# A hybrid trunk layer: the row tiles of the last two attention heads and of the output projection, taken from the last to the first

## The chip, the cores and the metric

One NeuronCore of a Trainium2 chip runs the whole kernel; nothing is shared with other cores. The metric is the device time of one execution in microseconds (us). Of the kernel before there are three timed runs with a median of 576.46 us (576.36 to 576.82), and one profiled execution.

TensorE (PE) multiplies, VectorE (DVE), ScalarE (ACT) and GpSimd (POOL) do the element-wise work, and SyncE (SP) issues the transfers. Each engine works through its own list of instructions in the order in which they were written down, and waits where a result of another engine is not there yet.

## What is computed

One layer over 1024 positions of width 1024, batch 1, everything in 32-bit floats:

```
h    = rms_norm(x) * gain * (1 + scale(c)) + shift(c)
proj = h @ w_in                       # 1024 x 3328: state-space, 4 diff heads, sliding-window heads, gates
y    = concat( s5(u)             * silu(z_ssm),      # 256 columns
               diff_attention(q, k, v) * silu(z_diff),   # 4 heads x 128 columns
               sliding_window(q, k, v) * silu(z_swa) )   # 256 columns
out  = rms_norm(x + gate(c) * (y @ w_out))
```

A differential head takes two softmaxes over the same causal rows and subtracts them:

```
p = softmax(q1 k1' / 8 + bias) - lam * softmax(q2 k2' / 8 + bias)    # causal: query t sees keys 0..t
o = rms_norm(p @ v) * gain
```

Query tile i (128 positions) sees i + 1 key tiles, so tile 7 has eight times the keys of tile 0. Each tile of each head is independent of the others; a tile of `out` needs that tile of y from all heads.

## The kernel before

The program text is Python that writes the five instruction lists once, in an order that a small planner sets. A `Model` keeps an estimated clock for each engine and each tile. Every stage that belongs to attention, state space or epilogue is a generator; it yields what it waits for, and a `Mixer` resumes one when the model says that its inputs are there. TensorE's long matrix products (`proj`, the output projection) call `mix.tick()` between groups of three matmuls, and in these places the generators put their instructions. So the order on every engine depends on the model's clocks, and moving one stage moves many instructions. All instructions go through one helper, so the profile gives line 109 for all of them; the tiles' names tell them apart.

Products are exact to nearly 32 bits: an operand is split into a high and a low part (`woh` and `wol` of the output weights, `yh` and `yl` of y), and three matmuls go to each product.

The projections run in a fixed order, ending with z2, q3, k3, z3 (gate of head 2, queries and keys of head 3, gate of head 3). After a head's keys, `diff(h, i, ...)` is put in the mixer for its eight query tiles ("rows" below, i + 1 key tiles each); at most three rows of a head are under way. A row's steps and names:

- `pS`: scores on TensorE, in one or two pieces of up to 512 keys for each of the two softmaxes, four matmuls for a piece of both
- `sp`: DVE adds the bias and takes the row maximum in one pass per piece, ACT takes the exponential, DVE combines the two softmaxes
- `pdT`, `dT`: i + 1 transposes on TensorE, copied out by ACT (first four) and DVE (the rest)
- `pdO`: the product with v; `do`, `oo`: copy and square on ACT, then three small instructions on POOL (`dmx`), then DVE scales `do`
- `pdy`: transpose on TensorE, after which DVE multiplies the gate into `z`, which now holds this row of y

During z3, `on_k(k)` splits the output weights one 128-row tile after the other, in the order `KO`: ACT makes `woh`, and POOL (four tiles, in pieces of 256 columns) or DVE makes `wol`. The first two y tiles are loaded there too (`load_y`, six 128 x 128 pieces and the residual x) and split (`split_y`): six eighths come from memory, the last two eighths directly from the gates `z` of heads 2 and 3, once `DF[h]["done"]` counts enough rows.

The output projection runs in eight row tiles of two halves of 512 columns (the last tile in 512, 256, 256); up to three halves are open at once, and the loop takes one whose next eighth is ready. Where none is, it opens another or steps the mixer. A half takes 24 matmuls (`po`), eight times `woh*yh`, `wol*yh`, `woh*yl`. `epilogue` adds gate and residual on DVE (`res`), takes the norm and stores the tile.

What sets the order around the change is this loop with the mixer, the row counter `st["run"]` of each head and `done`, which the projection waits on.

Of the kernel before, what the change touches and what calls it, by code (L numbers as in the profile page):

```python
# [16 lines left out]
D = 1024  # L17
NT = 8
# [211 lines left out]
def body(ctx, tc, x, c, norm_gain, ada_w, ada_b, w_in, w_out, lam_re, lam_im, log_step,  # L230
# [45 lines left out]
    def when(cond):  # L276
        return lambda: 0.0 if cond() else 1e9
# [150 lines left out]
    PW = {}  # L428
# [890 lines left out]

    DF = {h: {"run": 0, "done": 0} for h in range(4)}  # L1320

    def diff(h, i, q, k, store, width):
        st = DF[h]
        yield (when(lambda: st["run"] == i and i - st["done"] < width and f"vn{h}" in VN and h in PW.get("bd", ())),
               k[0], k[1], k[2], k[3], q[1], VN.get(f"vn{h}", k[3]), bank("ps"))
        vn = VN[f"vn{h}"]
        bias = PW["bd"][h]
        if i == 6 and h < 3:
            PW["bd"][h + 1] = page(f"bd{h + 1}")
            g_scale(PW["bd"][h + 1], bias, 0.5)  # L1330
        ncol = (i + 1) * 128
        qs = slice(i * 128, (i + 1) * 128)
        if i < 4:
            t = page("sp", (128, 2, 512))
            sp = [t[:, m] for m in range(2)]
        else:
            sp = [page(f"sp{m}") for m in range(2)]
        mx = sml.tile([128, 8], F32, name="dmx", bufs=8)
        nch = (ncol + 511) // 512
        w = (i + 1 + nch - 1) // nch * 128  # L1340
        for a in range(nch):
            for m in range(2):
                if a or m:
                    yield (bank("ps"),)
                c0, c1 = a * w, min(ncol, (a + 1) * w)
                p = pst("ps", "pS")
                scores(p[:, :c1 - c0], q, k, m, qs, slice(c0, c1))
                o = 896 - 128 * i
                V.tensor_tensor_reduce(sp[m][:, c0:c1], p[:, :c1 - c0], bias[:, o + c0:o + c1], 0.125,
                                       -1e38 if a == 0 else mx[:, m:m + 1], OP.add, OP.max, mx[:, m:m + 1])  # L1350
                rel(p)
        st["run"] += 1
        V.tensor_scalar(mx[:, 2:4], mx[:, 0:2], -1.0, None, op0=OP.mult)
        yield (mx,)
        for m in range(2):
            A.activation(sp[m][:, :ncol], sp[m][:, :ncol], AF.Exp, bias=mx[:, 2 + m:3 + m],
                         accum_out=mx[:, 4 + m:5 + m])
        yield (sp[1], mx)
        V.reciprocal(mx[:, 6:8], mx[:, 4:6])
        V.scalar_tensor_tensor(mx[:, 0:1], mx[:, 7:8], mx[:, 4:5], nl, op0=OP.mult, op1=OP.mult)  # L1360
        V.scalar_tensor_tensor(sp[0][:, :ncol], sp[1][:, :ncol], mx[:, 0:1], sp[0][:, :ncol],
                               op0=OP.mult, op1=OP.add)
        pT = page("dT_", (128, 8, 128))
        for b0 in range(0, i + 1, 4):
            nb = min(4, i + 1 - b0)
            yield (sp[0], bank("pt"))
            p = pst("pt", "pdT", (128, 4, 128))
            for a in range(nb):
                PE.transpose(p[:, a], sp[0][:, (b0 + a) * 128:(b0 + a + 1) * 128], ident)
            if b0 == 0:  # L1370
                A.activation(pT[:, b0:b0 + nb], p[:, :nb], AF.Copy)
            else:
                V.tensor_copy(pT[:, b0:b0 + nb], p[:, :nb])
            rel(p)
        yield (pT, bank("po"))
        p = pst("po", "pdO", (128, 128))
        for a in range(i + 1):
            PE.matmul(p, lhsT=pT[:, a], rhs=vn[:, a], start=(a == 0), stop=(a == i))
        yield (p,)
        o = sml.tile([128, 128], F32, name="do", bufs=5)  # L1380
        oo = sml.tile([128, 128], F32, name="oo", bufs=2)
        A.activation(o, p, AF.Copy)
        rel(p)
        A.activation(oo, o, AF.Square, scale=mx[:, 6:7], accum_out=mx[:, 1:2])
        rsqrt(mx[:, 2:3], mx[:, 1:2], 128)
        G.tensor_tensor(mx[:, 3:4], mx[:, 2:3], mx[:, 6:7], OP.mult)
        yield (mx, "V")
        V.tensor_scalar(o, o, mx[:, 3:4], None, op0=OP.mult)
        yield (when(lambda: "z" in st),)
        z = st["z"]  # L1390
        yield (o, bank("pt"), z)
        p = pst("pt", "pdy", (128, 128))
        PE.transpose(p, o, ident)
        yield (p,)
        V.scalar_tensor_tensor(z[:, qs], p, subh, z[:, qs], op0=OP.mult, op1=OP.mult)
        rel(p)
        st["done"] += 1
        if store and st["done"] == NT:
            SP.dma_start(ycat[2 + h], z)
# [67 lines left out]
    def load_y(i):  # L1467
        t = page("yt", (128, 6, 128))
        for j, k in enumerate(KO[:6]):
            SP.dma_start(t[:, j], ycat[k][:, i * 128:(i + 1) * 128])  # L1470
        YT[i] = t
        XR[i] = page("xr")
        SP.dma_start(XR[i], dap(x, i * 128 * D, [[D, 128], [1, D]]))

    def split_y(i):

        yield (YT[i], when(lambda: i < 2 or DONE["po"] >= i - 1)) + (("A", "V") if i else ())
        t = YT.pop(i)
        hi = page("yh", (128, 8, 128), F32R)
        lo = page("yl", (128, 8, 128), F32R)  # L1480
        A.activation(hi[:, 0:6], t, AF.Copy)
        V.tensor_sub(lo[:, 0:6], t, hi[:, 0:6].bitcast(F32))
        SPL[i] = [hi, lo, [mdl.w[lo.tensor.name]] * 6]
        for j in range(2):
            yield (when(lambda: 2 + j in YD and DF[2 + j]["done"] > i),)
            yield (YD[2 + j],)
            y = YD[2 + j][:, i * 128:(i + 1) * 128]
            A.activation(hi[:, 6 + j], y, AF.Copy)
            V.tensor_sub(lo[:, 6 + j], y, hi[:, 6 + j].bitcast(F32))
            SPL[i][2].append(mdl.w[lo.tensor.name])  # L1490
# [57 lines left out]
    def epilogue(i, pp):  # L1548

        r = page("res")  # L1550
        ss2 = sml.tile([128, 4], F32, name="fs")
        jk = page("jk2")
        for n in range(2):
            cs_ = slice(n * 512, (n + 1) * 512)
            yield (when(lambda: len(pp) > n and DONE["n"] >= 2 * i + n + 1),)
            yield (pp[n], XR[i])
            tts(r[:, cs_], pp[n], gate["g"][:, cs_], OP.mult)
            DONE["h"] += 1
            tts(r[:, cs_], r[:, cs_], XR[i][:, cs_], OP.add)
            yield (r, "A")  # L1560
            A.activation(jk[:, cs_], r[:, cs_], AF.Square, accum_out=ss2[:, n:n + 1])
        yield (ss2,)
        tts(ss2[:, 2:3], ss2[:, 0:1], ss2[:, 1:2], OP.add, G)
        G.tensor_scalar(ss2[:, 2:3], ss2[:, 2:3], D * EPS, None, op0=OP.add)
        tts(ss2[:, 3:4], ss2[:, 2:3], mhalf, OP.pow, G)
        for n in range(2):
            yield (ss2, "V")
            cs_ = slice(n * 512, (n + 1) * 512)
            V.scalar_tensor_tensor(r[:, cs_], r[:, cs_], ss2[:, 3:4], gate["f"][:, cs_], op0=OP.mult, op1=OP.mult)
            SP.dma_start(dap(out, i * 128 * D + n * 512, [[D, 128], [1, 512]]), r[:, cs_])  # L1570

    def epilogue_last(i, pp, cols):

        r, jk = page("res"), page("jk2")
        ss2 = sml.tile([128, 8], F32, name="fl")
        G.memset(ss2[:, 0:1], D * EPS)
        for n, c in enumerate(cols):
            yield (when(lambda: len(pp) > n and DONE["n"] >= 2 * i + n + 1),)
            yield (pp[n], XR[i])
            tts(r[:, c], pp[n], gate["g"][:, c], OP.mult)  # L1580
            tts(r[:, c], r[:, c], XR[i][:, c], OP.add)
            if n < 2:
                yield (r, "A")
                A.activation(jk[:, c], r[:, c], AF.Square, accum_out=ss2[:, n + 4:n + 5])
                tts(ss2[:, n + 1:n + 2], ss2[:, n:n + 1], ss2[:, n + 4:n + 5], OP.add, G)
            else:
                V.tensor_tensor_reduce(jk[:, c], r[:, c], r[:, c], 1.0, ss2[:, 2:3], OP.mult, OP.add, ss2[:, 3:4])
            tts(r[:, c], r[:, c], gate["f"][:, c], OP.mult)
        tts(ss2[:, 6:7], ss2[:, 3:4], mhalf, OP.pow, G)
        yield (ss2,)  # L1590
        c0, c1 = cols[0], slice(cols[1].start, cols[2].stop)
        A.activation(r[:, c1], r[:, c1], AF.Copy, scale=ss2[:, 6:7])
        V.tensor_scalar(r[:, c0], r[:, c0], ss2[:, 6:7], None, op0=OP.mult)
        for c in (c0, c1):
            SP.dma_start(dap(out, i * 128 * D + c.start, [[D, 128], [1, 512]]), r[:, c])

    mix.until(lambda: "f" in gate)
    half = [slice(0, 512), slice(512, 1024)]
# [66 lines left out]
```

## Time and profile before

| | |
|---|---|
| timed runs, median (range) | 576.46 us (576.36 to 576.82) |
| profiled execution: its time | 576.38 us |
| its span, first to last instruction | 574.6 us |
| granted TensorE clock, mean | 0.991 |
| last TensorE matmul starts | 567.72 us into the span |
| matmuls on TensorE | 3170 |

The engines' busy times overlap. Matmuls are pipelined: a group of n starts a matmul every 0.23 us for 512 columns, though each is shown with 0.39 us. All lists below are in us from the start of the span. z3 runs from 439.1 to 454.5, the output projection from 454.5 to 567.9.

### The profile page before, as it was taken

The numbers are of one execution on the slowest core, as the hardware profiler recorded it, in microseconds if no ns is written. First come the engines' busy times: TensorE is split into PE (matmuls) and PEld (weight loads), VectorE is DVE, ScalarE is ACT, GpSimd is POOL, SyncE is SP. The second block draws the span as 40 slices with busy tenths as digits, with TensorE's granted clock in tenths as the row PEclk, the third lists the DMA queues.
The fourth block names the chain that finished last, engine by engine and source line by source line (L and its number), as shares of the span: only waits on it lengthen the run. The fifth ranks groups of instructions, "written<-read, shape, count | busy, mean of one in ns | idle before, by whom it ended". The sixth has DMA issues, their size and how long they took to land.

```text
span 574.6 us, 9274 instructions
## 1 busy us (share of the span) xinstructions
PE 552.6 (96%) x3170; PEld 462.4 (80%) x3170; DVE 407.6 (71%) x1061; ACT 262.3 (46%) x595; POOL 191.3 (33%) x348
## 2 busy tenths in 40 slices
PE   8999999999689999999999999999999999799995
PEld 6667888888578997787788889998888887688885
DVE  4886886995879656778766768734867967866434
ACT  5545221151614346444645765635548735632211
POOL 3354242010306046362466172414341932210011
PEclk9999999999979999999999999999999999999998
DMA  8993076003411340356320111005216603024211
GB/s 292 353 351 86 3 195 135 0 2 37 115 38 37 59 145 1 131 208 220 97 88 2 37 38 38 2 1 146 75 30 194 190 27 98 31 75 144 96 38 73
DMA packets 60075, 56.42 MB, mean 98 GB/s; under 512 B 13088, under 2 KB 52315, under 8 KB 60027
## 3 DMA queue, kind: packets, MB, share of 16 engines
q1 hardware_dynamic: 58806, 55.54, 31.8%
q10 hardware_dynamic: 1220, 0.28, 0.5%
q8 instruction: 25, 0.41, 0.3%
q14 instruction: 24, 0.19, 0.1%
HBM read 45.78 MB, written 9.44 MB: 96 GB/s over the span
## 4 chain that ended last, share of the span: by engine, by line
PE 61%; DVE 5%; ACT 3%; issue 3%; POOL 2%; ACTq 1%; POOLq 0%; DVEq 0%
PE po L109 13%; PE p_z L109 8%; PE p_v L109 7%; PE p_k L109 7%; PE pdO L109 5%; PE p_q L109 5%; PE pS L109 5%; PE pdT L109 3%; PE pY L109 2%; PE pwO L109 1%; PE pG L109 1%; PE psw L109 1%; PE pwT L109 1%; DVE sp L109 1%; PE p_qs L109 1%
## 5 line engine op out<-in xcount | busy, mean ns | idle before, releaser
L109 ACT ACTIVATE sp<-sp,dmx 128x128 f32<-128x128 f32 (+7 forms) x64 | 49.0, 768 | 16.5 <-DVE dmx L109 15.4
L109 PE MATMUL po<-woh,yh 128*128 128x512 f32 (+1 forms) x136 | 52.2, 384 | 1.1 <-ACT yh L109 1.1
L109 PE MATMUL po<-wol,yh 128*128 128x512 f32 (+1 forms) x136 | 51.5, 378 | 0.5 <-POOL wol L109 0.5
L109 PE MATMUL po<-woh,yl 128*128 128x512 f32 (+1 forms) x136 | 51.4, 378 | 0.0
L109 POOL TENSOR_SCALAR dmx<-dmx 128x1 f32<-128x1 f32 x32 | 8.1, 252 | 109.3 <-ACT oo L109 108.5
L109 DVE CUSTOM_DVE_ANT_0 sp<-pS,bd 128x384 f32<-128x384 f32 (+3 forms) x64 | 33.7, 552 | 10.7 <-PE pS L109 10.5
L109 PE MATMUL p_v<-wh_v,hh 128*128 128x256 f32 x128 | 37.8, 295 | 0.0
L109 PE MATMUL p_v<-wh_v,hl 128*128 128x256 f32 x128 | 36.2, 283 | 0.0
L109 PE MATMUL p_v<-wl_v,hh 128*128 128x256 f32 x128 | 36.1, 282 | 0.0
L109 POOL TENSOR_TENSOR swp<-swp,swm 128x256 f32<-128x256 f32 x30 | 19.9, 696 | 37.7 <-DVE swm L109 28.6
L109 ACT ACTIVATE jk<-res 128x512 f32<-128x512 f32 (+1 forms) x16 | 9.9, 616 | 46.5 <-DVE res L109 46.5
L109 PEld LDWEIGHTS po<-woh,yh 128*128 128x128 f32 x136 | 25.6, 188 | 5.9 <-ACT yh L109 1.5
L109 PEld LDWEIGHTS po<-wol,yh 128*128 128x128 f32 x136 | 25.6, 188 | 5.2 <-POOL wol L109 1.0
L109 PEld LDWEIGHTS po<-woh,yl 128*128 128x128 f32 x136 | 25.6, 188 | 4.9 <-DVE yl L109 0.2
L109 PE MATMUL p_k<-hh,wh_k 128*128 128x512 f32 x64 | 26.4, 413 | 0.0
L109 PE MATMUL p_q<-hh,wh_q 128*128 128x512 f32 x64 | 26.1, 407 | 0.0
L109 PE MATMUL p_z<-hh,wh_z 128*128 128x512 f32 x64 | 25.7, 402 | 0.0
L109 PE MATMUL p_q<-hh,wl_q 128*128 128x512 f32 x64 | 25.1, 393 | 0.0
L109 PEld LDWEIGHTS p_v<-wh_v,hh 128*128 128x128 f32 x128 | 24.4, 191 | 0.9 <-issue 0.8
L109 PE MATMUL p_k<-hh,wl_k 128*128 128x512 f32 x64 | 25.1, 393 | 0.0
L109 PE MATMUL p_q<-hl,wh_q 128*128 128x512 f32 x64 | 25.1, 392 | 0.0
L109 PE MATMUL p_z<-hl,wh_z 128*128 128x512 f32 x64 | 25.0, 391 | 0.0
(487 smaller groups left out, 1663.0 us busy)
## 6 DMA issues: line engine op xcount, KB each, us to landing
aw<-in_ada_w_dram SPq DMA_DIRECT2D x32, 256.0 KB
x<-in_x_dram SPq DMA_DIRECT2D x8, 512.0 KB
gaw<-in_ada_w_dram SPq DMA_DIRECT2D x8, 512.0 KB
wo<-in_w_out_dram SPq DMA_DIRECT2D x8, 512.0 KB
xr<-in_x_dram SPq DMA_DIRECT2D x8, 512.0 KB
out_dram<-res SPq DMA_DIRECT2D x16, 256.0 KB
yt<-ycat SPq DMA_DIRECT2D x48, 64.0 KB
wr_z<-in_w_in_dram SPq DMA_DIRECT2D x4, 512.0 KB
```

The source lines that it names most:

```text
L109: return f(*args, **kw)
```

## The change

For heads 2 and 3 the rows are taken 7, 6, ..., 0 instead of 0, 1, ..., 7; heads 0 and 1 are as before. The output projection, its loads and its stores go through the row tiles in the same reversed order, so that its first tile is the one whose attention rows come first.

```
+    turned = lambda i: NT - 1 - i
+
-    def diff(h, i, q, k, store, width):
+    def diff(h, r, q, k, store, width):
+
         st = DF[h]
+        i = r if h < 2 else turned(r)
-        yield (when(lambda: st["run"] == i and i - st["done"] < width and ...
+        yield (when(lambda: st["run"] == r and r - st["done"] < width and ...
...
-        if i == 6 and h < 3:
+        if r == 6 and h < 3:
...
-            SP.dma_start(t[:, j], ycat[k][:, i * 128:(i + 1) * 128])
+            SP.dma_start(t[:, j], ycat[k][:, turned(i) * 128:(turned(i) + 1) * 128])
...
-        SP.dma_start(XR[i], dap(x, i * 128 * D, [[D, 128], [1, D]]))
+        SP.dma_start(XR[i], dap(x, turned(i) * 128 * D, [[D, 128], [1, D]]))
...
-            y = YD[2 + j][:, i * 128:(i + 1) * 128]
+            y = YD[2 + j][:, turned(i) * 128:(turned(i) + 1) * 128]
...
-            SP.dma_start(dap(out, i * 128 * D + n * 512, [[D, 128], [1, 512]]), r[:, cs_])
+            SP.dma_start(dap(out, turned(i) * 128 * D + n * 512, [[D, 128], [1, 512]]), r[:, cs_])
```

Since the planner sets the order, the text of the change does not show what moves. Below are pieces of the lists, where `x8` stands for eight equal instructions in a row. `sp_` and `dT_` with a number are the tiles of one row; `pS` with `128x512` or `128x384` is a piece of scores.

TensorE, before, in the middle of the output projection (row tile 1, head 3's rows 5 to 7):

```order
L109 MATMUL po_4996<-woh_4773,yl 128x512
L109 MATMUL pdT<-ident,sp_5055 128x128 x6
L109 MATMUL pS<-k3m_4442,q3m_4241 128x384
L109 MATMUL pS<-k3m_4444,q3m_4241 128x384
L109 MATMUL pS<-k3m_4443,q3m_4242 128x384
L109 MATMUL pS<-k3m_4445,q3m_4242 128x384
L109 MATMUL pdy<-ident,do 128x128
L109 MATMUL pdO<-vn_3627,dT__5150 128x128 x6
```

TensorE, after, from where row tile 7 of the projection has used up what needs no head 3 (rows 6 and 5 of head 3):

```order
L109 MATMUL po_4859<-woh_4782,yl 128x512
L109 MATMUL pdO<-vn_3627,dT__4875 128x128 x8
L109 MATMUL pS<-k3m_4534,q3m_4297 128x384
L109 MATMUL pS<-k3m_4536,q3m_4297 128x384
L109 MATMUL pS<-k3m_4535,q3m_4298 128x384
L109 MATMUL pS<-k3m_4537,q3m_4298 128x384
L109 MATMUL pdT<-ident,sp_4845 128x128 x7
L109 MATMUL pdy<-ident,do 128x128
```

Before, the big rows stood late, between groups of six projection matmuls of tiles whose rows were done; now they come at the start of the output projection, with only its first tile open.

DVE, after, a little further on (head 3's rows 5 to 3; `bd_` is the bias, `po_4821` and `po_4859` are the two halves of the first row tile):

```order
L109 SCALAR_TENSOR_TENSOR sp_4913<-sp_4914,dmx,sp_4913 128x768
L109 ISA sp_4987,dmx<-pS,bd_4497,dmx 128x256
L109 ISA dmx 128x1
L109 TENSOR_SCALAR dmx<-dmx 128x2
L109 TENSOR_TENSOR res<-po_4821,gbc 128x512
L109 TENSOR_TENSOR res<-res,xr 128x512
L109 TENSOR_SCALAR do<-do,dmx 128x128
L109 COPY dT__5024<-pdT 128x256
```

The scores of row 4 and the epilogue of the first half stand between row 5's combination and row 6's `do`.

ACT, before, behind the copies of k3:

```order
L109 ACTIVATE k3m_4443<-k3m_4443 64x512
L109 ACTIVATE woh_4640<-wo_4446 128x1024
L109 ACTIVATE yh<-yt 128x768
L109 ACTIVATE yh<-z_4082 128x128
L109 ACTIVATE dT__4619<-pdT 128x512
L109 ACTIVATE woh_4679<-wo_4448 128x1024
```

and after:

```order
L109 ACTIVATE k3m_4535<-k3m_4535 64x512
L109 ACTIVATE do<-pdO 128x128
L109 ACTIVATE oo,dmx<-do,dmx 128x128
L109 ACTIVATE woh_4668<-wo_4538 128x1024
L109 ACTIVATE yh<-yt 128x768
L109 ACTIVATE yh<-z_4082 128x128
L109 ACTIVATE woh_4695<-wo_4540 128x1024
```

The copy of head 2's row 7 is gone from between the first two weight tiles (that row is long done), and the last row of head 2 (row 0) stands ahead of them.

More of the change, by code (lines that the diff above doesn't have):

```diff
@@ L1320, in body @@
     DF = {h: {"run": 0, "done": 0} for h in range(4)}
-    def diff(h, i, q, k, store, width):
+    turned = lambda i: NT - 1 - i
+    def diff(h, r, q, k, store, width):
         st = DF[h]
-        yield (when(lambda: st["run"] == i and i - st["done"] < width and f"vn{h}" in VN and h in PW.get("bd", ())),
+        i = r if h < 2 else turned(r)
+        yield (when(lambda: st["run"] == r and r - st["done"] < width and f"vn{h}" in VN and h in PW.get("bd", ())),
                k[0], k[1], k[2], k[3], q[1], VN.get(f"vn{h}", k[3]), bank("ps"))
@@ L1594, in epilogue_last @@
         for c in (c0, c1):
-            SP.dma_start(dap(out, i * 128 * D + c.start, [[D, 128], [1, 512]]), r[:, c])
+            SP.dma_start(dap(out, turned(i) * 128 * D + c.start, [[D, 128], [1, 512]]), r[:, c])
     mix.until(lambda: "f" in gate)
```

## The prediction

> **What bounds the kernel now.** First the page's head and its busy shares:
>
> ```profile
> span 574.6 us, 9274 instructions
> PE 552.6 (96%) x3170; PEld 462.4 (80%) x3170; DVE 407.6 (71%) x1061; ACT 262.3 (46%) x595; POOL 191.3 (33%) x348
> ```
>
> TensorE is busy for 96% of the span, and a new order of the same work moves little but its idle time. Which of it the change can touch is read from the windows, cut at the stages (us, then PE, PEld, DVE, ACT and POOL busy):
>
> ```profile
> 386.50:438.40 51.90, 51.72 (x282) 43.80 (x281) 34.08 (x106) 30.36 (x74) 17.71 (x34) 1.00 0.32 99
> 438.40:454.50 16.10, 16.10 (x90) 13.88 (x89) 14.89 (x31) 12.33 (x23) 10.94 (x15) 1.00 0.60 178
> 454.50:466.40 11.90, 11.36 (x61) 9.28 (x60) 8.30 (x17) 5.82 (x20) 8.35 (x13) 1.00 0.40 124
> 476.90:499.10 22.20, 18.16 (x114) 15.69 (x113) 17.17 (x50) 13.77 (x36) 5.29 (x12) 1.00 0.26 83
> 514.00:567.80 53.80, 53.80 (x261) 45.49 (x259) 27.52 (x46) 11.26 (x31) 6.09 (x18) 1.00 0.26 84
> ```
>
> The projection z3 (438 to 454) has no gap, and neither has the output projection once attention is done (514 to 568). Between them TensorE idles while DVE works 17.2 of 22.2 us. The waits of TensorE from 454 to 515:
>
> ```profile
> PE pdy L109 <- DVE do L109: 2.6, 1, 2.6
> PE po L109 <- ACT yh L109: 1.1, 1, 1.1
> PE po L109 <- POOL wol L109: 0.5, 1, 0.5
> PE pdT L109 <- DVE sp L109: 0.4, 1, 0.4
> ```
>
> They sum to 4.6 us: all that the change can remove here. How the longest one arises stands in the chain of waits (start, us, engine and tile):
>
> ```profile
> 489.99 2.17 ACT sp L109 x4
> 492.64 1.81 DVE sp L109 x2
> 494.46 0.66 DVE sp L109
> 495.33 0.60 DVE res L109
> 497.12 0.21 DVE do L109
> 497.46 0.30 PE pdy L109
> ```
>
> The value `do` that TensorE needs stands on DVE's queue behind the scores of two other rows and behind an epilogue (`res`). DVE runs in the order written, and TensorE too, so a chain of a few big rows serializes both. The question is how many big rows of head 3 meet how much projection work.
>
> **The change, part by part.** Nothing is added or removed: matmuls, vector work and transfers are those of before, and SP's queue brings row 7's y and x first instead of row 0's. What moves is the order.
>
> Head 2 and z3: the big rows of head 2 now come first, between projections that need nothing from them; in the new order three or more projection matmuls stand between most of the row steps. I take 0 us here. The bounds: TensorE's gaps from 386.5 to 438.4 are 0.2 us (the first window), which could go; a stall as long as the mean of the four above, 1.1 us, could come.
>
> Splitting the output weights. Their split starts when k3's halves are out, and k3's end comes later: head 2's last rows no longer stand behind it, but before it.
>
> ```profile
> 439.07 0.39 PE L109 MATMUL p_z<-hh,wh_z 128*128 128x512 f32 x1
> 454.50 0.48 PE L109 MATMUL po<-woh,yh 128*128 128x512 f32 x1
> 443.70 0.60 ACT L109 ACTIVATE dT__4619<-pdT 128x512 f32<-128x512 f32 x1
> 444.19 3.89 ACT L109 ACTIVATE woh<-wo 128x1024 fp32r<-128x1024 f32 x4
> 506.33 0.28 ACT L109 ACTIVATE do<-pdO 128x128 f32<-128x128 f32 x1 [3.12 <-PE pdO L109]
> 507.04 0.83 ACT L109 ACTIVATE yh<-yt 128x768 fp32r<-128x768 f32 x1
> 445.32 7.66 POOL L109 TENSOR_TENSOR wol<-wo,woh 128x256 fp32r<-128x256 f32 x8 [4.49 <-ACT woh L109]
> 453.06 0.19 POOL L109 TENSOR_SCALAR dmx<-dmx 128x1 f32<-128x1 f32 x1
> 454.11 7.30 POOL L109 TENSOR_TENSOR wol<-wo,woh 128x256 fp32r<-128x256 f32 x8
> ```
>
> TensorE's net prices for the rest, from the chain again:
>
> ```profile
> 502.13 0.88 PE pdT L109 x8
> 504.50 1.79 PE pdO L109 x16
> 485.25 0.93 PE pS L109 x4
> 483.87 1.39 PE po L109 x6
> ```
>
> Before, k3's end (439.07) lies 15.4 us ahead of the output projection (454.50). Now only z3's 48 matmuls (48 x 1.39/6 = 11.1) and row 7's eight score matmuls (2 x 0.93) lie between: 13.0. With the start of the projection kept at 454.5, k3 ends 2.4 us later. On ACT the second weight tile followed 5.12 us after it (444.19); now a dT copy in between is gone (-0.49) and a `do` with its square is added (507.04 - 506.33 = +0.71). POOL, which began 1.13 us behind that tile, begins at 439.07 + 2.4 + 5.34 + 1.13 = 448.0. It makes sixteen pieces of 256 columns at (7.66 + 7.30)/16 = 0.94 us; the first half of the row tile needs 14 of them, 13.1 us, so 461.1; the `dmx` triple that cut them in two is out of the way now. TensorE gets there after 18 projection matmuls (4.2), four scores (0.93) and one more (0.23): 459.8. **Wait: 1.3 us**, where 0.5 stood. Bounds: none, if the pieces ran as when POOL splits k's weights (first row here, 0.71 each, 14 in 9.9); the second row prices DVE's part:
>
> ```profile
> 403.12 1.43 POOL L109 TENSOR_TENSOR wl_k<-wr_k,wh_k 128x256 fp32r<-128x256 f32 x2 [1.73 <-ACT wh_k L109]
> L109 DVE TENSOR_TENSOR yl<-yt,yh 128x768 fp32r<-128x768 f32 x5 | 4.8, 955 | 3.7 <-ACT yh L109 3.5
> ```
>
> Upward: twice my value, 2.6.
>
> The Trainium skill ("SBUF — State Buffer", section "SBUF: two separate sides") has a rule against the change here: DVE with two SBUF inputs and GpSimd hold a common port pair by an exclusive lock, and the other one blocks fully. DVE has three weight subtractions of 1024 columns and one copy there in the new order, an estimated 3 x 1.2 + 0.7 = 4.3 us by the 955 ns of the 768-wide yl. By that rule POOL would need 9.9 + 4.3 = 14.2 us, the wait would be 2.4 us and the time 582.0. The trace of before agrees that POOL is slowed (13.1 us for 14 pieces, 3.2 above the quick ones, while DVE was busy 14.9 of 16.1 us), but not by how much each lock costs.
>
> Head 3's big rows. Row tile 7 now comes first in the projection. After seven eighths of its sum both its halves need head 3's row 7, and the next tile's y is split only behind four rows of scores. From row 7's transposes (call that moment P: 461.1, then 20 projection matmuls, 4.6, two pdy and four scores, 1.0: about 466.7) to the first matmul of tile 6, TensorE's queue holds 26 transposes (2.8), the scores of rows 5, 4 and 3 (3.8, by width from the 0.93 of 512), three pdO groups (42 matmuls, 4.7), two pdy (0.3) and eleven projection matmuls up to the one that needs yl (2.5): **14.1 us of work**. DVE's queue for the same stretch, by its groups (mean ns):
>
> ```profile
> L109 DVE CUSTOM_DVE_ANT_0 sp<-pS,bd 128x512 f32<-128x512 f32 x12 | 7.9, 687 | 3.0 <-PE pS L109 3.0
> L109 DVE CUSTOM_DVE_ANT_0 sp<-pS,bd 128x384 f32<-128x384 f32 x12 | 6.2, 549 | 0.0
> L109 DVE CUSTOM_DVE_ANT_0 sp<-pS,bd,dmx 128x384 f32<-128x384 f32 x8 | 4.7, 616 | 0.4 <-PE pS L109 0.4
> L109 DVE SCALAR_TENSOR_TENSOR sp<-sp,dmx,sp 128x896 f32<-128x896 f32 x2 | 2.3, 1152 | 0.1
> L109 DVE SCALAR_TENSOR_TENSOR sp<-sp,dmx,sp 128x768 f32<-128x768 f32 x2 | 2.0, 1019 | 0.1
> L109 DVE SCALAR_TENSOR_TENSOR sp<-sp,dmx,sp 128x640 f32<-128x640 f32 x2 | 1.9, 971 | 0.1
> L109 DVE TENSOR_TENSOR res<-res,xr 128x512 f32<-128x512 f32 x6 | 4.2, 692 | 0.2
> L109 ACT ACTIVATE sp<-sp,dmx 128x512 f32<-128x512 f32 x4 | 2.9, 716 | 3.9 <-DVE dmx L109 3.9
> ```
>
> With 0.08 off for the overlap of neighbours: ten score passes 5.0, three combinations of the two softmaxes 2.9 with 1.3 for their scalars, four `res` 2.6, yl 0.9, and 3.1 for three dT copies, `do`, z and sign changes (estimates by width from these rows, as is the 256-wide pass): 15.8 us. The first can start 1.1 us after P, so P to tile 6 takes at least 16.9 us: **a floor of 2.8 us** of new stall, if DVE never waits. It will wait, since scores come only in TensorE's order. The walk, in us after P, with 0.15 per hand-over (in the chain, pdy starts at 497.46, 0.13 behind the end of `do`) and a score pass 0.6 behind its scores' start (half of the 0.93 and a hand-over):
> - Row 6's transposes: TensorE arrives at 0.8 + 0.8 + 0.7 + 1.7 + 0.8 = 4.8 (transposes, scores, projection, pdO, scores). The combination of row 6 stands on DVE behind row 5's second scores, issued at 4.0: 4.6 + 0.54 + 1.5 = 6.75. Wait 2.1; row 7's pdy then 0.15.
> - Row 5's transposes: TensorE resumes at 6.9 and does 0.7 + 0.3 + 0.8 + 1.5 + 0.3 + 0.7 + 0.3 + 0.7 = 5.2 or so: arrival 12.1; DVE has row 4's scores from 10.65, then 0.4 + 1.4: 12.65. Wait 0.55.
> - Row 6's pdy: arrival 13.2; `do` stands behind a score pass, a sign change and two `res` (0.6 + 1.3 + 0.2): 14.75. Wait 1.5.
> - Row 4's transposes: arrival 14.75 + 0.1 + 0.95 + 1.3 = 17.1 (pdy, scores, pdO); ahead on DVE are row 3's two passes (from 15.6, 1.2), a sign change (0.2), two `res` (1.3) and the combination (1.3): 19.75. Wait 2.65.
> - Tile 6: ACT splits y behind row 3's exponentials (2 x 0.7), DVE then makes yl, 21.2. Wait 0.6; two short ones behind it 0.25.
>
> **Sum 7.8 us.** I take the walk, not the floor, because the chain of before shows just this queueing. Upper bound: the walk plus its longest wait again, 10.5.
>
> **Total.** -4.6 removed, +1.3 for the weights, +7.8 for the rows: +4.5 us. Afterwards rows 3 to 0 are small against the projection beside them, and the end is unchanged work: 0. The profiled execution took 576.38 us for its span of 574.6; the span becomes 579.1 and the time 580.9. It stands 0.08 below the median of the runs, which I leave.
>
> **Rivals.**
> - *The floor holds.* DVE packs well, weights are in time: -4.6 + 2.8 = -1.8, so 574.6; with no stall at all 571.8. For it: small rows at the end need little, as 514 to 568 shows. Against it: the 2.6 us wait of before, with DVE at 77%. 0.13.
> - *The stall only moves.* New waits between 3.5 and 5.7 us in place of 4.6: 576.4. 0.11.
> - *Worse than the walk.* Once the walk's longest wait (2.65) occurs twice, as would happen if an ACT exponential also came behind a dT copy it has to wait for, and the weights at their upper bound: -4.6 + 2.6 + 10.5 = +8.5, 584.9. For it: ACT's exponentials are queued behind transposes. Against it: my walk already holds those orders. 0.10.
> - *Forecast*, new waits between 5.8 and 12: 0.66.
>
> **How the numbers follow.** About 0.2% (1.15 us) is what a measurement of this kernel tells from no change. Forecast and worse case are slower, 0.76; the moved stall is the same, 0.11; the floor is faster, 0.13. The range runs from 576.0, which leaves out the faster case and little else, to 584.0, below the worst case. The forecast alone: 578 to 583.
>
> **What would show it.** Right: in the waits of TensorE from 454 on, pdT on DVE sp and pdy on DVE do sum to 6 us or more, most between 465 and 490; POOL's first `wol` starts near 448 and one wait on it exceeds 1 us; no gaps after 500. Wrong: TensorE's busy share between 465 and 490 above 85%, or new gaps before 450, where I put none. It would be wrong as a whole if DVE were ahead of TensorE at P and after.

## The result, and the profile after

The changed kernel takes 583.17 us (median of 4 runs, 582.23 to 584.95), the kernel before 576.64 us beside it (4 runs, 576.36 to 577.92). The ratio is 1.0104, with a 95% interval of 1.0078 to 1.013: slower by about 6.5 us. The forecast was 580.9 us, in a range of 576.0 to 584.0. The execution that was profiled is the longest of the four, 584.95 us for a span of 583.2. One single execution further down, the eighth of ten with head 3 and the projection alone, took 1108.47 us at a granted clock of 1.00 for a reason that no profile shows; the ratio there leaves it out.

The head of its page and the busy shares:

```profile
span 583.2 us, 9282 instructions
PE 556.8 (95%) x3170; PEld 465.6 (80%) x3170; DVE 408.1 (70%) x1061; ACT 261.9 (45%) x595; POOL 191.3 (33%) x348
```

The span is 8.6 us longer than before. TensorE's busy time grew by 4.2 us although its 3170 matmuls are the same ones: the added time is partly idle time, partly slower matmuls. The windows show where (us, then PE, PEld, DVE, ACT and POOL busy, the granted clock, the share of DMA, GB/s):

```profile
386.50:438.40 51.90, 51.89 (x298) 44.72 (x297) 35.29 (x105) 28.86 (x69) 17.69 (x34) 1.00 0.29 90
438.40:454.50 16.10, 16.10 (x76) 13.26 (x75) 11.30 (x19) 12.75 (x24) 8.05 (x11) 1.00 0.62 194
454.50:466.40 11.90, 10.53 (x48) 8.16 (x47) 10.90 (x22) 3.48 (x6) 9.68 (x12) 1.00 0.46 142
466.40:490.00 23.60, 17.41 (x104) 15.18 (x102) 16.21 (x49) 11.66 (x31) 3.65 (x9) 0.93 0.13 39
490.00:515.00 25.00, 24.61 (x128) 20.79 (x129) 16.19 (x51) 12.53 (x43) 5.91 (x16) 0.93 0.06 22
515.00:576.00 61.00, 61.00 (x294) 51.26 (x293) 32.40 (x56) 14.67 (x42) 8.48 (x24) 1.00 0.30 98
```

From 386.5 to 454.5 there is no gap, and none after 515. From 466.4 to 490 TensorE works 17.4 of 23.6 us (74%) and in two rows the granted clock is 0.93. All waits of TensorE from 380 to 525 in the changed kernel:

```profile
PE pdT L109 <- DVE sp L109: 4.9, 3, 2.5
PE po L109 <- POOL wol L109: 1.4, 2, 0.9
PE pdy L109 <- DVE do L109: 1.3, 1, 1.3
PE pdy L109 <- ACT dT__4956 L109: 0.4, 1, 0.4
```

They sum to 8.0 us where 4.6 stood before: +3.4. Each of them, from TensorE's timeline (the bracket holds the idle time just before the instruction):

```profile
460.06 0.50 PE L109 MATMUL po<-wol,yh 128*128 128x512 f32 x1 [0.49 <-POOL wol L109]
462.84 0.51 PE L109 MATMUL po<-wol,yh 128*128 128x512 f32 x1 [0.89 <-POOL wol L109]
475.35 0.95 PE L109 MATMUL pdT<-ident,sp 128*128 128x128 f32 x7 [1.98 <-DVE sp L109]
476.67 0.33 PE L109 MATMUL pdy<-ident,do 128*128 128x128 f32 x1 [0.36 <-ACT dT__4956 L109]
483.23 0.85 PE L109 MATMUL pdT<-ident,sp 128*128 128x128 f32 x6 [0.49 <-DVE sp L109]
485.35 0.30 PE L109 MATMUL pdy<-ident,do 128*128 128x128 f32 x1 [1.28 <-DVE do L109]
490.39 0.75 PE L109 MATMUL pdT<-ident,sp 128*128 128x128 f32 x5 [2.47 <-DVE sp L109]
```

The other part is the clock. Four windows, cut by hand where the granted clock changes (us, PE busy, granted clock, DMA share, GB/s):

```profile
473.91:477.32 3.41, 1.61 (x11) 1.00 0.41 142
477.32:480.74 3.42, 3.42 (x18) 0.50 0.01 2
487.58:490.99 3.41, 0.94 (x10) 1.00 0.00 0
490.99:494.40 3.41, 3.41 (x11) 0.50 0.02 5
```

Behind the waits of 1.98 and 2.47 us TensorE runs at half its clock for 3.4 us. Each time that costs 1.7 us, since 3.4 us of time hold 1.7 us of work at full rate: 3.4 us for both. So the profile reads +3.4 in waits and +3.4 in clock, 6.8 us, beside the 6.5 us by which the medians differ. The rest of the 8.6 us of span is 1.8 us. Half of it stands in the first 25 us of the span, where the same matmuls run in both kernels: there TensorE waits 1.3 us for ACT's `xt` in this execution, 0.4 us in the one before, and in most of the profiles below not at all. The other half was not traced.

### The profile page after: what moved, and what is told of

It reads as the page before. It is cut to its first block, busy times and chain, and to the rows that moved or that the text cites. A ratio compares the mean times of both kernels' runs of the same rounds, so it can differ in the third digit from the quotient of the medians.

```text
span 583.2 us, 9282 instructions
## 1 busy us (share of the span) xinstructions
PE 556.8 (95%) x3170; PEld 465.6 (80%) x3170; DVE 408.1 (70%) x1061; ACT 261.9 (45%) x595; POOL 191.3 (33%) x348
## 4 chain that ended last, share of the span: by engine, by line
PE 59%; DVE 8%; issue 3%; ACT 3%; POOL 1%; ACTq 1%; POOLq 0%; DVEq 0%
PE po L109 13%; PE p_v L109 7%; PE p_k L109 6%; PE p_z L109 6%; PE pdO L109 5%; PE p_q L109 5%; PE pS L109 5%; PE pdT L109 3%; DVE sp L109 2%; PE pY L109 2%; PE pwO L109 1%; PE pG L109 1%; PE psw L109 1%; PE pwT L109 1%; PE p_qs L109 1%
## 5 line engine op out<-in xcount | busy, mean ns | idle before, releaser
L109 PE MATMUL pdT<-ident,sp 128*128 128x128 f32 x144 | 21.3, 274 | 5.4 <-DVE sp L109 5.3
```

The lines of the kernel that those rows point to most:

```text
L109: return f(*args, **kw)
```

## The experiments

Every run is compared with the kernel before on the same chip, and the ratios say by how much. The medians come from different chips, on which the kernel before took 575.97 to 576.64 us, so a difference between two medians of these runs is good to about 1 us. In the diffs, `ROWS_` lists the rows of heads 2 and 3 in the order in which they are taken, and `PO_` the row tiles of the projection; the change itself is 7 to 0 for all three. What the split of y waits for follows the same lists. The first four runs ask whether each reversal alone loses time, whether the half-rate clock comes from the idle time, and whether an earlier split of the second row tile's y mends the loss.

**Head 2 alone.**

```
ROWS_ = {2: [7, 6, 5, 4, 3, 2, 1, 0], 3: [0, 1, 2, 3, 4, 5, 6, 7]}
PO_ = [0, 1, 2, 3, 4, 5, 6, 7]
```

> Only head 2's rows are reversed; head 3 and the output projection go from the first row to the last as before. My theory (the cost is the chain of head 3's big rows at the start of the projection, with nothing else for TensorE): the weight split still starts 2 to 3 us later, so up to 1.4 us of wait on wol, and the waits on head 3's rows stay about those of before (4 to 5 us): 577 to 579 us. Rival 1 (head 2's reversal, by the late k3 and weight split, carries the loss): 581 us or more, with over 4 us of waits on wol. Rival 2 (it needs both reversals together): 576.5.

Measured: 575.72 us, ratio 0.9995 (0.9978 to 1.0013). No difference. TensorE's waits from 440 to 525:

```profile
PE pdT L109 <- DVE sp L109: 2.3, 1, 2.3
PE pdy L109 <- DVE do L109: 0.6, 1, 0.6
PE po L109 <- POOL wol L109: 0.6, 1, 0.6
```

They sum to 3.5 us, a little less than before, and one half-rate stretch from 510 takes the gain. Head 2's reversal loses nothing by itself; my expectation of a loss was wrong.

**Head 3 and the projection alone.**

```
ROWS_ = {2: [0, 1, 2, 3, 4, 5, 6, 7], 3: [7, 6, 5, 4, 3, 2, 1, 0]}
PO_ = [7, 6, 5, 4, 3, 2, 1, 0]
```

> Head 2 as before; head 3's rows and the output projection reversed. The written order now has a second row tile of the projection open beside the big rows (po matmuls in sixes between the steps of rows 7 to 4). My theory, in the form that big rows cost only where TensorE has nothing else: waits of 3 to 5 us from 454 on, none on wol over 0.6 us, clock at 1.00 throughout, 575.5 to 578 us. Rival 1 (big rows first are themselves the cost): waits of 6 us or more on pdT and pdy, 581 us or more.

Measured: 572.78 us (572.63 without the long execution), ratio 0.9939 (0.9918 to 0.996): faster than before, and below the 575.5 to 578 us that I expected. Its only wait between 440 and 525:

```profile
PE po L109 <- DVE z L109: 1.9, 1, 1.9
```

and the window that had 6 us of gaps in the change:

```profile
466.40:490.00 23.60, 23.60 (x145) 20.40 (x144) 16.92 (x54) 12.58 (x35) 3.60 (x11) 1.00 0.13 40
```

The big rows of head 3 at the start of the projection do not cost time as such. The loss needs both reversals.

**Idle time filled.** Eight, two and ten matmuls whose result nobody uses, written ahead of the transposes of head 3's rows 6, 5 and 4; all else is the order of the change.

```
+    FILL = {6: 8, 5: 2, 4: 10}
...
             p = pst("pt", "pdT", (128, 4, 128))
+            if h == 3 and b0 == 0 and i in FILL:
+                for _ in range(FILL[i]):
+                    nc.tensor.matmul(p, lhsT=onr, rhs=onr[:, None, :].to_broadcast([128, 4, 128]), start=True, stop=True)
```

> The changed kernel, with 8, 2 and 10 extra matmuls of ones (128 x 512) into the bank that the transposes of head 3's rows 6, 5 and 4 overwrite next: they fill TensorE's idle time there and are used by nobody; the order of all else is that of the change. Theory 1 (the granted clock fell to 0.67 and 0.70 at 476 to 480 and 492 to 496 because TensorE had idled 2 to 2.5 us): clock 1.00 in these stretches, the matmuls after them at 0.23 us again, 580 to 581 us, 2 to 3 us less than the change. Rival (the clock falls by itself, or by load): the same 0.93 over 466 to 515, 583 us or more.

Measured: 580.18 us, ratio 1.0062 (1.0041 to 1.0083), 3.0 us below the change by the medians (2.4 by the ratios) with more work in it. The window over the whole region:

```profile
452.00:515.00 63.00, 59.61 (x323) 1.00 0.16 51
```

The clock stays at 1.00. This is not only the profiled execution: the mean granted clock is 0.990 to 0.993 in all seven, and 0.985 to 0.988 in the four of the change. So the half rate follows the idle time and is worth 2 to 3 us here.

**The second tile's y split as soon as it is there.**

```
-        yield (YT[i], when(lambda: i < 2 or DONE["po"] >= i - 1)) + (("A", "V") if i else ())
+        yield (YT[i], when(lambda: i < 2 or DONE["po"] >= i - 1)) + (("A", "V") if i > 1 else ())
```

> The changed kernel, but the split of the second row tile's y no longer waits, in the planner, for ACT's and DVE's queues to be short; so row tile 6 can be opened between head 3's rows 7 and 6. My theory (TensorE lacked other work there): waits on pdT and pdy from 454 on fall from 6.6 us to 2 to 4, the clock stays above 0.97, 577 to 580 us. Rival 1 (DVE is the bound in this stretch and the split only adds to its queue): waits stay at 6 us or more, 582 us or more.

Measured: 581.74 us, ratio 1.0094 (1.0063 to 1.0124). The largest of its waits from 440 to 525:

```profile
PE po L109 <- POOL wol L109: 3.0, 2, 1.8
PE po L109 <- DVE res L109: 1.6, 1, 1.6
PE po L109 <- DVE yl L109: 1.0, 1, 1.0
```

No transposes wait for `sp` any more, but with three smaller waits these sum to 7.3 us. Now the split stands among the weight subtractions (DVE starts yl 1.4 us before the projection's first matmul), and the wait for the weights grew from 1.4 to 3.0, with a half-rate stretch behind it. POOL's sixteen pieces of weights take 15.5 us there for 14.8 in the change, and row 6's scores, which stand between the two waits in the change, come later; that both follow from the early split is argued, not shown by a run of its own. My expectation of the time was wrong: the rows' waits went, and others took their place.

The next four ask what of head 2's order matters, and price one step of the walk.

**DVE's queue.** The second `res` addition (the residual x) of the first half and of the second half of the first row tile is not issued; the planner's clocks are advanced as if it were, so the rest stands as in the change. The kernel leaves out the residual of that row tile.

```
-            tts(r[:, cs_], r[:, cs_], XR[i][:, cs_], OP.add)
+            if i:
+                tts(r[:, cs_], r[:, cs_], XR[i][:, cs_], OP.add)
+            else:
+                V.tensor_tensor.account(r[:, cs_], r[:, cs_], XR[i][:, cs_], OP.add)
```

> The changed kernel with the residual left out for the first row tile of the projection (row tile 7): the two DVE additions of xr, 0.69 us each, that stand between row 5's combination and row 6's do and between row 3's scores and row 4's combination are not issued; the rest of the order is that of the change. My theory (TensorE waits there for DVE's queue in the order written): the wait of pdy on do falls from 1.3 to about 0.6 us, that of row 4's transposes from 2.5 to 1.5 to 1.9; with a second slow-clock stretch perhaps spared, 580 to 582.5 us. Rival (the waits come from the score and softmax chain itself, and the epilogue only uses DVE's spare time): both waits stay within 0.2 us, 583 us.

Measured: 581.95 us, ratio 1.008 (1.0054 to 1.0105). Row 6's pdy and row 4's transposes:

```profile
481.86 0.31 PE L109 MATMUL pdy<-ident,do 128*128 128x128 f32 x1 [0.55 <-ACT dT__5024 L109]
486.17 0.74 PE L109 MATMUL pdT<-ident,sp 128*128 128x128 f32 x5 [1.74 <-DVE sp L109]
```

The two waits that had one `res` addition ahead of them each fell by 0.73 us (1.28 to 0.55, 2.47 to 1.74), where one such addition takes 0.69; the waits of 1.98, 0.36 and 0.49 us ahead of them did not move. So these two are time on DVE's queue, and the prediction's way of counting them holds.

**Head 2 with small rows last, with big rows last, and with row 7 in the middle**; head 3 and the projection reversed in all three.

```
ROWS_[2] = [2, 3, 4, 5, 6, 7, 1, 0]     # small rows last
ROWS_[2] = [5, 4, 3, 2, 1, 0, 6, 7]     # big rows last
ROWS_[2] = [0, 1, 2, 3, 7, 4, 5, 6]     # row 7 in the middle
```

> Head 3 and the projection reversed; head 2's rows in the order 2, 3, 4, 5, 6, 7, 1, 0, so that small rows are what head 2 leaves for z3. Theory A (what counts is how much DVE has to do during z3: work missing there comes back later as waits): DVE busy under 12.5 of the 16 us from 438 to 454, waits of 5 us or more from 454 on, 578 us or more. Theory B (what counts is the written order at the start of the projection: here row 7's transposes stand behind 27 projection matmuls, not 42, and a second tile is opened before row 6's transposes are copied): waits under 4 us, 573 to 576 us in spite of DVE's idle time in z3.

> Head 3 and the projection reversed; head 2's rows in the order 5, 4, 3, 2, 1, 0, 6, 7, so that big rows are what head 2 leaves for z3. Theory A (DVE's work during z3 counts): DVE busy 14 us or more of the 16 from 438 to 454, waits of 3 us or less, 572 to 575 us. Theory B (the written order counts: here only the first row tile is open until after row 5's product with v): waits of 5 us or more on pdT and pdy, 577 us or more.

> Head 3 and the projection reversed; head 2's rows in the order 0, 1, 2, 3, 7, 4, 5, 6, so that row tile 7's y does not wait for head 2's last row (the one wait of 1.9 us in the version with head 2 unchanged). If that wait just goes: 570 to 572 us. If the planner's new order takes it back elsewhere: 572.5 to 576 us. Theory A puts it near the version with head 2 unchanged, since DVE still has big rows during z3.

Measured: 572.72 us, ratio 0.9923 (0.9892 to 0.9954); 572.51 us, 0.9916 (0.9886 to 0.9946); 573.26 us, 0.9924 (0.9897 to 0.9951). All three are faster than before. Neither theory survives: by A the first should have been slow, by B the second. (For A this run alone is not enough, since DVE was busy for 12.9 of the 16.1 us from 438.4, a little above the 12.5 that A named; in the last run below it is busy for 11.9 at 573.68 us.) With row 7 in the middle the wait of 1.9 us on z is gone, and the time stays all the same. Even the order 2 to 7, 1, 0, whose end is that of the change, has no waits of head 3's rows. What the change has and these do not was found by counting, in the written order, the projection matmuls between the first transposes of head 3's row 7 and those of its row 4: 9 in the change, 33 to 45 in the fast orders. The reason is the second row tile: until its y is split, nothing of it can be multiplied. In the changed kernel DVE makes that yl at

```profile
490.93 0.96 DVE L109 TENSOR_TENSOR yl<-yt,yh 128x768 fp32r<-128x768 f32 x1 [0.69 <-ACT yh L109]
```

which is 35.1 us after the projection's first matmul, behind the scores of four rows; in the fast orders it is 18 to 25 us after it. Two theories were left: *C*, head 3's first scores are late and the first row tile is used up before row 7's transposes (39 of its 48 matmuls stand ahead of them, against 27 with small rows last); *D*, the missing matmuls in between.

**Scores late, filler kept.** The order 2 to 7, 1, 0, with head 3's first scores held back to where the change has them.

```
+    WR = {"po": 0, "z": 0, "sc": 0}
...
-        yield (when(lambda: st["run"] == r and ...
+        yield (when(lambda: not (h == 3 and r == 1 and WR["po"] < 18)),
+               when(lambda: st["run"] == r and ...
...
-                    yield (bank("ps"),)
+                    yield (bank("ps"), when(lambda: not (h == 3 and r == 0 and a and not WR["z"])))
```

> Head 3's rows and the projection reversed, head 2's rows in the order 2 to 7, 1, 0 (573 us so far), and the scores of head 3's row 7 (second half) held back until the gate projection has ended, those of row 6 until 18 projection matmuls are written, as they stand in the changed kernel. Row 7's transposes then have 39 projection matmuls ahead of them, as in the changed kernel (27 without the hold), but up to row 4's transposes 36 more follow (9 in the changed kernel). Theory C: the loss comes from head 3's first scores being late, so that the first row tile is used up: 579 us or more, with waits of the transposes on DVE of 3 us or more. Theory D: the loss comes from the few projection matmuls between the big rows' transposes, because the next row tile is not open there: 571 to 576 us, transposes' waits below 2 us.

Measured: 577.82 us, ratio 1.0025 (1.001 to 1.0041). All waits from 440 to 525:

```profile
PE po L109 <- POOL wol L109: 3.7, 1, 3.7
PE po L109 <- DVE res L109: 0.9, 1, 0.9
```

No transposes wait, as D has it, but the time is outside both forecasts. Of the 5 us above the kernel without the hold, 4.3 are a longer wait for the weights (3.7 for 2.0), a half-rate stretch behind it (1.7) and 0.9 us on `res`.

**Scores early, filler missing.** The change, with the second scores of row 7 and the first of row 6 written earlier.

```
+        if k == 7:
+            mix.until(lambda: WR["sc"] >= 4)
         split_wo(KO[k])
...
         u[3] += 1
+        WR["po"] += 3
+        if WR["po"] == 9:
+            mix.until(lambda: WR["sc"] >= 6)
```

> The changed kernel, but row 7's second scores are written before the last eighth of the gate projection has split its weights, and row 6's first scores after 11 projection matmuls instead of 18; from row 7's transposes on the order is that of the change, with 9 projection matmuls up to row 4's transposes. Theory C: clearly faster than the change, 580 us or less. Theory D: 581.5 to 584 us, the three waits of the transposes on DVE still 4 to 5 us in sum and the clock still halved behind them.

Measured: 583.15 us, ratio 1.0118 (1.0082 to 1.0154). Three rows of TensorE's timeline:

```profile
474.45 0.95 PE L109 MATMUL pdT<-ident,sp 128*128 128x128 f32 x7 [1.98 <-DVE sp L109]
482.78 0.30 PE L109 MATMUL pdy<-ident,do 128*128 128x128 f32 x1 [1.28 <-DVE do L109]
487.82 0.74 PE L109 MATMUL pdT<-ident,sp 128*128 128x128 f32 x5 [2.47 <-DVE sp L109]
```

and the window over the region:

```profile
452.00:515.00 63.00, 54.57 (x302) 1.00 0.17 53
```

These waits are those of the change to the hundredth, though the scores come earlier: C falls. D's "clock still halved" was not seen in this profile, where the clock is 1.00 throughout; that execution took 581.26 us at a mean granted clock of 0.991. The other three of this kernel took 583.10 to 583.39 us, all at 0.985, as three of the change's four executions: 0.006 of some 580 us is 3.5 us, what the two half-rate stretches cost the change. So it fits D in three executions of four, though their stretches themselves were not profiled.

**The second tile's y split in between.** One condition of the changed kernel: the split comes when 24 projection matmuls are written (`WR["po"]` counts them).

```
-        yield (YT[i], when(lambda: i < 2 or DONE["po"] >= i - 1)) + (("A", "V") if i else ())
+        yield (YT[i], when(lambda: i < 2 or DONE["po"] >= i - 1)) + ((when(lambda: WR["po"] >= 24),) if i == 1 else ("A", "V") if i else ())
```

> The changed kernel with one condition replaced: the second row tile's y is split when 24 projection matmuls are written, instead of when VectorE and ScalarE are free by the planner's clocks. Up to row 7's transposes TensorE's order stays that of the change (39 projection matmuls ahead of them, row 6's scores after 18); up to row 4's transposes 36 projection matmuls follow instead of 9. Theory D (the loss comes from that missing work, because the second tile's y is split 35 us into the projection): the transposes' waits on DVE fall from 4.9 us to below 1, sum of all waits below 3 us, no half-rate clock after 470, time 574 to 577 us, equal to the kernel before or faster. Rival (the late start of head 3's rows, or VectorE's queue as such, would still hold them): transposes' waits 3 us or more, 580 us or more. Rival (another wait takes their place, as when the split was not delayed at all): 579 to 582 us.

Measured: 573.68 us, ratio 0.9958 (0.9943 to 0.9972): 9.5 us below the change by the medians (8.4 by the ratios), faster than the kernel before, and a little below the 574 to 577 us that I expected. DVE's yl of the second tile, on its timeline:

```profile
464.69 0.96 DVE L109 TENSOR_TENSOR yl<-yt,yh 128x768 fp32r<-128x768 f32 x1
```

All waits of TensorE from 440 to 525:

```profile
PE po L109 <- POOL wol L109: 1.3, 2, 0.9
PE po L109 <- DVE res L109: 0.9, 1, 0.9
```

And the window of the gaps:

```profile
466.40:490.00 23.60, 22.58 (x141) 19.57 (x139) 16.86 (x51) 13.38 (x35) 3.58 (x9) 1.00 0.13 40
```

The projection begins at 453.01, so the split comes 11.7 us into it. Row 7's transposes still have 39 matmuls ahead of them, as in the change; 36 instead of 9 follow up to row 4's. The transposes' waits go from 4.9 us to none, all waits from 8.0 to 2.2, the clock stays at 1.00. The 5.8 us of waits and the 3.4 us of clock make 9.2 us. From z3's first matmul (443.08 in the change, 440.29 here) to the end of the span, the two profiles differ by 9.0 us. D is confirmed with the smallest edit. The kernels beside one another:

| kernel | second tile's yl, us after the projection's first matmul | projection matmuls between the transposes of rows 7 and 4 | transposes' waits on `sp`, us | all waits, us | median, us |
|---|---|---|---|---|---|
| change | 35.1 | 9 | 4.9 | 8.0 | 583.17 |
| scores early | 33.5 | 9 | 4.9 | 8.5 | 583.15 |
| split at once | -1.4 | 48 | 0 | 7.3 | 581.74 |
| scores late | 1.0 | 36 | 0 | 4.6 | 577.82 |
| split at 24 | 11.7 | 36 | 0 | 2.2 | 573.68 |
| head 2 as before | 18.7 | 42 | 0 | 1.9 | 572.78 |
| small rows last | 19.9 | 39 | 0 | 2.0 | 572.72 |
| big rows last | 25.2 | 45 | 0 | 1.2 | 572.51 |
| row 7 in the middle | 17.7 | 33 | 0 | 0.6 | 573.26 |

Too late, the rows have no cover; at once, among the weights, other waits stand in the place of theirs. The best of these kernels are 0.8% faster than the one before; their intervals overlap, so none of them is singled out.

## Why the prediction was right

**The direction and the mechanism** were right: the rows of head 3 wait on DVE with hardly any projection work between them, because the next tile's y is split behind four rows of scores. The sentence on that split is what the experiments found to be the cause.

**The walk**, step by step:

| step | predicted wait, us | measured, us |
|---|---|---|
| weights (`wol`) | 1.3 | 0.49 + 0.89 |
| row 6's transposes | 2.1 | 1.98 |
| row 7's pdy | 0.15 | 0.36 |
| row 5's transposes | 0.55 | 0.49 |
| row 6's pdy | 1.5 | 1.28 |
| row 4's transposes | 2.65 | 2.47 |
| tile 6's yl and two short ones | 0.85 | 0 |
| sum | 9.1 | 8.0 |

Row 7's transposes start at 468.46, 12.7 us after the projection's first matmul (12.2 by the prediction), and row 6's 6.9 us behind them, as the walk has it. The queue that the prediction counted ahead of row 6's `do` and row 4's combination, on DVE's timeline of the change:

```profile
483.00 0.47 DVE L109 CUSTOM_DVE_ANT_0 sp<-pS,bd,dmx 128x256 f32<-128x256 f32 x1
...
483.60 0.68 DVE L109 TENSOR_TENSOR res<-po,gbc 128x512 f32<-128x512 f32 x1
484.32 0.69 DVE L109 TENSOR_TENSOR res<-res,xr 128x512 f32<-128x512 f32 x1
484.93 0.28 DVE L109 TENSOR_SCALAR do<-do,dmx 128x128 f32<-128x128 f32 x1
...
487.58 0.68 DVE L109 TENSOR_TENSOR res<-po,gbc 128x512 f32<-128x512 f32 x1
488.30 0.69 DVE L109 TENSOR_TENSOR res<-res,xr 128x512 f32<-128x512 f32 x1
...
489.36 0.89 DVE L109 SCALAR_TENSOR_TENSOR sp<-sp,dmx,sp 128x640 f32<-128x640 f32 x1
```

Tile 6 did not wait: its y was split while TensorE went through the matmuls ahead of it at half rate. With the clock at 1.00 (idle time filled, scores early) a wait on yl of 0.2 and 0.3 us stands there, so the last term of the walk, 0.85 us, was too large either way. Some sums of the walk are rough: 4.6 + 0.54 + 1.5 is 6.64 and not 6.75, 10.65 + 0.4 + 1.4 is 12.45 and not 12.65. With the 0.15 for a hand-over that it allows elsewhere they agree to 0.05 us.

**The weights** behaved as counted from the rows:

```profile
449.41 14.76 POOL L109 TENSOR_TENSOR wol<-wo,woh 128x256 fp32r<-128x256 f32 x16 [0.66 <-PE p_z L109]
```

POOL starts 6.4 us ahead of the projection (6.5 predicted), with 0.92 us for a piece (0.94). By the rule of an exclusive lock (the Trainium skill, "SBUF — State Buffer", section "SBUF: two separate sides"), 14 pieces were to take an estimated 14.2 us and the wait 2.4; the row gives 14 x 0.92 = 12.9 and the waits 1.4. The measurement decides: the lock, counted in full, was too dear. That there would be one wait of over 1 us was wrong; there are two shorter ones, with row 6's scores in between.

**The step that was off** is the total: "Total. -4.6 removed, +1.3 for the weights, +7.8 for the rows". Its sum of +4.5 is +3.4 in the trace, and a term is missing that it did not have: the clock. With the waits filled the kernel takes 580.18 us, and the one execution with these waits at full clock took 581.26, beside a forecast of 580.9. So the forecast holds for a kernel whose clock stays up. The 583.17 that was measured is above the 578 to 583 of the forecast alone, and in the whole range because that reached towards the upper rival, whose own reason (a second stall of 2.65 us) did not come. So the place inside the range is in part luck: waits counted 1.1 us too high stood in for a part of a clock loss of 3.4 us that was not counted at all.

**Head 2 and z3 at 0 us** was right as to gaps: none there in the windows above. But the prediction took the start of head 3 as given by the rows alone; it did not ask whether the late split depended on head 2's order, and the loss does: with head 2 as before, the same rows of head 3 gain 0.6%. Of how head 2's order moves the planner's clocks so that the split comes at 35 us instead of 18 to 25, nothing more was measured.

**The rivals.** The floor (574.6) and the moved stall (576.4) did not come. What kernels with head 3 and the projection reversed can reach, 572.5 to 573.7, is below the floor rival and near its "no stall at all", 571.8: the prediction held that case to depend on DVE's packing, and it depended on where one split is written.

## What to carry to other kernels

Where a planner sets the order, count in the written order how much independent work stands between the steps of a serial chain; 9 matmuls instead of 36 cost some 9 us here, and one condition on the split that opens the next tile gave them back. A change that loses may do so by a side effect of the planner: try its parts alone, since here neither part lost anything and their sum lost 1%. Price idle time of TensorE above its length, as the clock behind it may be halved.

## What the runs showed of the hardware

**Half rate stands on a grid.** The two half-rate stretches of the change last 3.4 us each and start at 477.32 and 490.99, 13.7 us apart, four times their length. The same trace has an earlier one of two lengths, long before the part that the change moves (us, PE busy, granted clock, DMA share, GB/s):

```profile
159.89:166.72 6.83, 5.31 (x25) 0.50 0.00 0
```

From its start to the one at 477.32 are 317.4 us, 93 times 3.413. In all 13 traces of this case every half-rate stretch starts a whole number of these lengths, to within 1% of one, after the first of its trace. So the early stretch, which every trace has, places the grid in each execution. In the windows on that grid just ahead of the change's two later stretches (shown above) TensorE worked 1.61 and 0.94 of 3.41 us. The Trainium skill ("TensorE: Matmul & The Clock Gate", section "What's actually happening") gives a free-running window of 3413 ns, with half rate after an idle one; in "Why this matters for your kernels" it asks for no idle gaps above some 3 us. The length and the grid agree with the trace; the limit does not: 1.80 and 2.47 us of idle time, in windows in which TensorE worked for 47 and 28% of the time, were enough.

**Where a gap lies on the grid counts, not its length alone.** The kernel before has a wait of 2.57 us and the one with small rows last one of 2.0, at a clock of 1.00; the run with the scores early has the three gaps shown for it, as long as those of the change, and no half rate in its profile. These are the windows on their grids that hold most of these gaps; the kernel before first, then scores early, then small rows last:

```profile
492.46:495.87 3.41, 2.06 (x12) 1.00 0.00 0
495.87:499.28 3.41, 1.82 (x16) 1.00 0.00 0
480.34:483.75 3.41, 1.82 (x11) 1.00 0.02 5
483.75:487.17 3.42, 1.60 (x14) 1.00 0.00 0
458.98:462.39 3.41, 1.57 (x7) 1.00 0.47 160
```

The edge at 495.87 cuts the wait of the kernel before in two, and TensorE works for 46 to 60% of the time in all five. Over all windows at full clock of the 13 traces, those with less than 44% were all followed by half rate and those with more than 57% never. In between both occur: 47% was enough in the change, and 47% was not with the scores early. What decides there is not shown. As the grid lies otherwise in each execution, the same program can lose 3.4 us in one and nothing in the next, which fits the four executions of the run with the scores early.
